# The second feed-forward product of a three-mixer block: from four full block products to seven, summed over the pairs of inner tiles

## The chip, the cores and the metric

One core of one Trainium2 chip runs the whole kernel. The metric is device time in microseconds (us) of one execution. The engines are PE (TensorE, matmuls), DVE (VectorE), ACT (ScalarE), POOL (GpSimd) and SP (SyncE, which here only issues DMAs). Each engine works through its own instructions in a fixed order, so an instruction that waits holds up all that stand behind it on that engine.

## The reference, cut to what matters

The kernel computes one layer of a hybrid backbone. The change touches its last part, the feed-forward block and the norm behind it (`lat` has 1024 tokens of 1024 channels; the hidden width is 2816):

```
def swiglu(xn, w_in, w_out):
    gate, up = jnp.split(xn @ w_in, 2, axis=-1)
    return (jax.nn.silu(gate) * up) @ w_out
...
h_lat = h_lat + gt2l * swiglu(modulate(rms_norm(h_lat, norm2), sh2l, sc2l), w_ffn_in, w_ffn_out)
...
return rms_norm(h_lat, norm_f)
```

The product by `w_in` is called the first product here, the one by `w_out` the second. The second is (1024 x 2816) by (2816 x 1024).

## The kernel before

Matmuls run on fp32r operands. To keep fp32 accuracy each operand is split into a high part (ACT writes a rounded copy, L1670) and a low part (DVE subtracts the copy from the raw tile, L1671), and each product of two tiles is three matmuls: high by high, high by low, low by high. One matmul is 128 x 128 by 128 x 512 and fills or adds to one of eight PSUM banks (tile `mm`).

`ffn_in` makes the hidden tensor, transposed: a tile is 128 hidden channels by 512 tokens. It goes by pairs of hidden tiles (11 pairs), and already uses a seven-product scheme for its own 2 x 2 blocks: per pair 2 x 7 products of 12 matmuls, gate and up. `done` applies SiLU to the gate tiles (L1598, ACT) and multiplies up by gate (L1601, POOL); `hidden(i, g)` sends the four finished tiles of pair i to the DRAM tensor `hid_d` (L1589, issued on SP). `g[j, h]` is hidden tile j of the pair and token half h.

`ffn_out` makes the second product. It loops over the two token halves h; in each half, for every one of the 22 hidden tiles k, it loads the hidden tile (L1676, tile `hraw`, four buffers) and the weight rows (L1681, tile `wraw`, 128 x 1024), splits the hidden tile into `hk` (six buffers) and the two weight halves into `wk` (`wt` for the first four k of the first half), and issues 24 matmuls (L1718): 4 token tiles t by 2 column halves n by 3. All eight banks are in use in a half. The weights are thus loaded and split twice. In the last two k the order is turned to t and n outside, k inside, so that the banks finish one after the other, and `out` follows each: multiply by the gate row `bc1` (L1689, DVE), add the residual (L1691, POOL, the last token tile on DVE), sum of squares (L1693, ACT), and after the second column half the root (L1699, L1700, POOL), the final norm (L1704, DVE) and the store (L1705).

The order on each engine comes from a scheduler at build time; pools hand out buffers, and DMAs are issued in program order on SP's queue, each waiting there for its buffer or its data. Pools are opened on the right side as others close, so the first tiles of `ffn_out` lie where `ffn_in` kept its data.

Of the kernel before, what the change touches and what calls it, by code (L numbers as in the profile page):

```python
# [16 lines left out]
P = 128  # L17
# [1076 lines left out]
RK, WK, HK = 4, 6, 6  # L1094
HR, WR = 4, 4
# [16 lines left out]
class Kern(LruMixin, S5Mixin, RwkvMixin, ParamMixin, SplitMixin):  # L1112
# [546 lines left out]
    def ffn_out(s, ring, wpool, apool, hpool, pa):  # L1659


        nc = s.nc
# [11 lines left out]
        def hidden(k, h):
            raw = hpool.tile([P, 512], F32, name="hraw", tag="hraw", bufs=HR)
            nc.sync.dma_start(raw, s.hid_d[k, h])  # L1676
            return operand(raw, hpool, "hk", HK)

        def weights(k, first):
            raw = pa.tile([P, D], F32, name="wraw", tag="wraw", bufs=WR)  # L1680
            nc.sync.dma_start(raw, s.i["w_ffn_out"][0][P * k : P * k + P, :])  # L1681
            pool, tag, bufs = (ring, "wt", 8) if first and k < RK else (wpool, "wk", 2 * WK)
            return [operand(raw[:, 512 * n : 512 * n + 512], pool, tag, bufs) for n in range(2)]

        def out(h, t, n, ps, rs):
            j = 4 * h + t
            at = lambda n: acc[:, j, 512 * n : 512 * n + 512]
            v = pa.tile([P, 512], F32, name="ot", tag="ot", bufs=4)
            V.tensor_tensor(v, ps, bc1[:, 512 * n : 512 * n + 512], op=ALU.mult)  # L1689
            a = at(n)  # L1690
            (V if h and t == 3 else G).tensor_tensor(a, a, v, op=ALU.add)  # L1691
# [290 lines left out]
```

## Time and profile before

| what | value |
| --- | --- |
| median of 3 runs | 2331.59 us (2330.96 to 2336.67) |
| the profiled execution's own time | 2331.55 us |
| its span in the profile | 2329.8 us |
| mean granted TensorE clock | 0.952 |

The profile shows one execution, with its times counted from the start of the span; the execution's own time is 1.75 us longer than the span. A busy time is the time in which an engine had at least one instruction under way. Idle time is put down to the releaser that came last.

### The profile page before, as it was taken

Reading aid. Unit: us, or ns where it says so; the run is one execution under the profiler, and the core shown is the slowest. Engines: PE = TensorE matmul, PEld = TensorE weight load, DVE = VectorE, ACT = ScalarE, POOL = GpSimd, SP = SyncE. Lnnn points to the kernel's source line nnn. Section 1 sums busy time; section 2 is a strip of 40 time slices with the busy share of each in tenths; the row PEclk is TensorE's granted clock in tenths of the full one; section 3 lists DMA queues with packets and bytes.
Section 4 is the critical chain, followed back from the end, with each engine's and each line's share of the span. In section 5 each row is a group of like instructions: output and inputs, shape, how many; then the busy total and the mean of one; then the engine's idle time right before and its main releaser. Section 6 shows DMA issues by size and latency. Waiting matters only on the chain.

```text
span 2329.8 us, 38390 instructions
## 1 busy us (share of the span) xinstructions
PE 2102.5 (90%) x14573; PEld 1675.7 (72%) x14573; DVE 1508.0 (65%) x2218; ACT 904.2 (39%) x1698; POOL 986.0 (42%) x1169
## 2 busy tenths in 40 slices
PE   5979988887899988898699999898999999989998
PEld 3868866665778877776467676676788888878886
DVE  5656698889566888899843366936855555543533
ACT  5313354423334645454533333416433323233431
POOL 3662389955323494856100122544644444300302
PEclk8989999998999999998699999998999999999999
DMA  6634322221663535445967777544222222274540
GB/s 254 168 110 115 90 66 83 82 84 64 143 174 89 161 111 140 125 136 142 246 181 173 171 191 183 167 158 136 81 77 86 77 86 77 68 276 151 165 149 36
DMA packets 360550, 307.26 MB, mean 132 GB/s; under 512 B 66023, under 2 KB 311982, under 8 KB 359342
## 3 DMA queue, kind: packets, MB, share of 16 engines
q1 hardware_dynamic: 356782, 293.27, 43.5%
q10 hardware_dynamic: 2880, 10.49, 1.2%
q8 instruction: 115, 1.88, 0.3%
q0 software_dynamic: 704, 1.05, 0.2%
q14 instruction: 69, 0.57, 0.1%
HBM read 219.03 MB, written 85.70 MB: 131 GB/s over the span
## 4 chain that ended last, share of the span: by engine, by line
PE 56%; DVE 19%; POOL 9%; DMA 7%; issue 5%; ACT 3%; SPq 1%; DVEq 0%; POOLq 0%; ACTq 0%
PE mm L1563 18%; PE mm L1718 10%; PE mm L1303 8%; PE mm L1309 7%; PE cg L1011 2%; PE cg L985 2%; PE cu L998 2%; DMA wm<-in_w_mod_dram 1%; DVE zl L1296 1%; PE cy L1026 1%; POOL s L214 1%; DVE s5ct L522 1%; PE aux L609 1%; DVE macc L1269 1%; DVE rn L748 1%
## 5 line engine op out<-in xcount | busy, mean ns | idle before, releaser
L1563 PE MATMUL mm<-q,wt 128*128 128x512 f32 x1584 | 376.6, 398 | 4.5 <-DVE q L1477 3.2
L1563 PEld LDWEIGHTS mm<-q,wt 128*128 128x128 f32 x1584 | 299.4, 189 | 77.5 <-DVE q L1477 3.6
L1718 PE MATMUL mm<-wk,hk 128*128 128x512 f32 x960 | 224.2, 396 | 0.0
L1303 PE MATMUL mm<-xh,wh 128*128 128x512 f32 (+1 forms) x576 | 214.4, 380 | 8.4 <-ACT ya L180 6.1
L1303 PE MATMUL mm<-xl,wh 128*128 128x512 f32 (+1 forms) x576 | 214.3, 379 | 1.2 <-DVE xl L1219 1.2
L1718 PEld LDWEIGHTS mm<-wk,hk 128*128 128x128 f32 x960 | 180.4, 188 | 43.6
L1309 PE MATMUL mm<-xh,zh 128*128 128x512 f32 x384 | 159.6, 416 | 10.0 <-ACT zge L1345 5.8
L1309 PE MATMUL mm<-xl,zh 128*128 128x512 f32 x384 | 159.5, 415 | 0.0
L1303 PE MATMUL mm<-xh,wl 128*128 128x512 f32 (+1 forms) x576 | 141.2, 383 | 8.8 <-DVE wl L1296 6.6
L1303 PEld LDWEIGHTS mm<-xh,wh 128*128 128x128 f32 x576 | 114.3, 199 | 28.6 <-ACT ya L180 6.9
L1671 DVE TENSOR_TENSOR wk<-wraw,wk 128x512 fp32r<-128x512 f32 x80 | 55.9, 707 | 111.3 <-ACT wk L1670 111.3
L1303 PEld LDWEIGHTS mm<-xl,wh 128*128 128x128 f32 x576 | 113.8, 197 | 19.4 <-DVE xl L1219 1.5
L1309 PE MATMUL mm<-byt,bwh 128*128 128x512 f32 x384 | 118.6, 428 | 7.9 <-ACT bwh L1295 2.9
L1303 PEld LDWEIGHTS mm<-xh,wl 128*128 128x128 f32 x576 | 102.9, 197 | 30.1 <-DVE wl L1296 8.2
L1309 PE MATMUL mm<-xh,zl 128*128 128x512 f32 x384 | 110.1, 423 | 15.3 <-DVE zl L1296 15.3
L1691 POOL TENSOR_TENSOR acc<-acc,ot 128x512 f32<-128x512 f32 x14 | 19.0, 1358 | 225.7 <-DVE ot L1689 225.2
L1015 DVE TENSOR_TENSOR x<-cg,pcend 64x256 f32<-64x256 f32 x152 | 63.9, 421 | 77.9 <-PE cg L1011 35.4
L1476 ACT ACTIVATE wt<-wT 128x512 fp32r<-128x512 f32 x88 | 55.1, 631 | 142.5 <-PE mm L1563 130.5
L1309 PEld LDWEIGHTS mm<-xh,zl 128*128 128x128 f32 x384 | 75.4, 202 | 35.2 <-DVE zl L1296 18.3
L1269 DVE SCALAR_TENSOR_TENSOR macc<-wm,cs,macc 128x256 f32<-128x256 f32 x112 | 84.6, 755 | 22.3 <-DMA wm<-in_w_mod_dram 19.8
L1477 DVE TENSOR_TENSOR wt<-wt 128x512 fp32r<-128x512 f32 x66 | 60.5, 918 | 59.4 <-ACT wt L1476 59.0
L1293 POOL CAST bwh<-bwr 128x512 fp32r<-128x512 f32 x16 | 10.0, 624 | 209.6 <-PE mm L1309 112.1
(421 smaller groups left out, 4865.3 us busy)
## 6 DMA issues: line engine op xcount, KB each, us to landing
wt<-in_w_ffn_in_dram SPq DMA_DIRECT2D x44, 512.0 KB
wraw<-in_w_ffn_out_dram SPq DMA_DIRECT2D x44, 512.0 KB
wm<-in_w_mod_dram SPq DMA_DIRECT2D x64, 256.0 KB
gyl<-gyl SPq DMA_DIRECT2D x32, 512.0 KB
wr<-in_w_in_dram SPq DMA_DIRECT2D x27, 512.0 KB
zr<-in_w_in_dram SPq DMA_DIRECT2D x24, 512.0 KB
sgd<-zge SPq DMA_DIRECT2D x48, 256.0 KB
bsg<-sgd SPq DMA_DIRECT2D x48, 256.0 KB
```

Source lines behind the costliest of these rows:

```text
L985: s.pe = nc.tensor.matmul(ps[32 * q : 32 * q + 32, 64 * p : 64 * p + 64], gy[:, 2 * p + par, c - cb, 0:32], st["x"][:, p, par, :], start=T ...
L998: s.pe = nc.tensor.matmul(ps[o : o + 32, 64 * p : 64 * p + 64], st["tt"][32 * q : 32 * q + 32, p, st["cc"], :], st["gs"][32 * q : 32 * q + ...
L1011: s.pe = nc.tensor.matmul(sn[64 * par : 64 * par + 64, 64 * p : 64 * p + 64], sd[:, st["cc"], 2 * p + par, :], st["x"][:, p, par, :], star ...
L1015: V.tensor_tensor(xn[0:64, :, par, :], sn[r].rearrange("p (a k) -> p a k", a=4), vb(s.pcend[r, d, :, st["c"]], 64), op=ALU.mult)
L1269: nc.vector.scalar_tensor_tensor(acc, wm[:, j], s.cs[:, k + j, 0:1], acc, op0=ALU.mult, op1=ALU.add)
L1303: s.nc.tensor.matmul(ps, w(k), a(k), start=n == 0, stop=n == len(seq) - 1)
L1309: s.nc.tensor.matmul(ps, w[:, k], a[:, k], start=n == 0, stop=n == len(seq) - 1)
L1476: s.nc.scalar.activation(hi, raw, AF.Copy)
L1477: (eng or s.nc.vector).tensor_tensor(lo, raw, hi, op=ALU.subtract)
L1563: nc.tensor.matmul(ps, w[:, k], a[:, k], start=n == 0, stop=n == len(seq) - 1)
L1671: V.tensor_tensor(hl[:, 1], raw, hl[:, 0], op=ALU.subtract)
L1718: nc.tensor.matmul(banks[t, n], a[:, tk], b, start=k == 0 and q == 0, stop=k == NF - 1 and q == 2)
```

## The change

`hidden` now sends seven tiles per pair instead of four: a11, a12, a21, a22 (first index token half, second index tile of the pair) and the sums a21 = a21 + a22, f2 = a21 - a11, f0 = a11 - a21 (before the sum), f1 = a12 - f2. The sums overwrite the gate tiles, which are kept for it (`g` holds both now). Two of the four extra operations are POOL's, two DVE's.

`ffn_out` runs seven products c = 0 to 6. Each multiplies one kind of hidden tile with one kind of weight block (128 x 512) over the 11 pairs k, for 4 token tiles t, three matmuls each, in four banks. The even c share one set of four banks and the odd c the other. Products 2, 4 and 6 are added to what the set holds. The 44 raw weight blocks are loaded once, each into its own buffer; the differences that products 1, 2, 4 and 6 need are made in place by POOL (`sub`). The split of operands moves to `split2` (L1475 on ACT, L1476 on DVE), all weight operands go through the `wt` ring (eight buffers), and the last two pairs of a product have t outside. `done(c, t)` takes a finished bank into `acc`; products 3 to 6 finish one quarter of the output each, for which `out` loads the residual itself (`xr`, two buffers, on SP; before it was loaded into `acc` on ACT's queue).

```diff
-            for (j, h), v in g.items():
-                nc.sync.dma_start(s.hid_d[2 * i + j, h], v)
+            (a11, f0), (a12, f1), (a21, _), (a22, f2) = g[0, 0], g[1, 0], g[0, 1], g[1, 1]
+            G.tensor_tensor(f0, a11, a21, op=ALU.subtract)
+            V.tensor_tensor(a21, a21, a22, op=ALU.add)
+            V.tensor_tensor(f2, a21, a11, op=ALU.subtract)
+            G.tensor_tensor(f1, a12, f2, op=ALU.subtract)
+            for c, v in enumerate((a11, a21, f2, a12, f0, f1, a22)):
+                nc.sync.dma_start(s.hid_d[c, i], v)
...
+        def block(k, j, n):
+            w = raw[k, j, n] = wpool.tile([P, 512], F32, name="wraw", tag=f"w{j}{n}{k}")
+            r = 2 * P * k + P * j
+            nc.sync.dma_start(w, s.i["w_ffn_out"][0][r : r + P, 512 * n : 512 * n + 512])
+            return w
...
+            if c == 0:
+                return block(k, 0, 0)
+            if c == 1:
+                return sub(w(0, 0), block(k, 0, 1), w(0, 0))
+            if c == 2:
+                return sub(w(0, 0), block(k, 1, 1), w(0, 0))
+            if c == 3:
+                return block(k, 1, 0)
+            if c == 4:
+                return sub(w(0, 1), w(1, 1), w(0, 1))
+            if c == 5:
+                return w(1, 1)
+            return sub(w(0, 0), w(1, 0), w(0, 0))
...
+        def out(h, n, t, v):
+            a, j = acc[:, h, n, t], 4 * h + t
+            x = pa.tile([P, 512], F32, name="xr", tag="xr", bufs=2)
+            nc.sync.dma_start(x, s.x2_d[j, :, 512 * n : 512 * n + 512])
+            E = V if (h, n) == (1, 0) else G
+            E.tensor_tensor(a, v, bc1[:, 512 * n : 512 * n + 512], op=ALU.mult)
+            (V if (h, n, t) == (1, 0, 3) else G).tensor_tensor(a, a, x, op=ALU.add)
...
+        def done(c, t):
+            ps = banks[c % 2][t]
+            if c < 2:
+                S.activation((o11, o21)[c][t], ps, AF.Copy)
+            elif c == 2:
+                S.activation(o12[t], ps, AF.Copy)
+                G.tensor_tensor(o12[t], o12[t], o21[t], op=ALU.add)
+            elif c == 3:
+                V.tensor_tensor(o11[t], o11[t], ps, op=ALU.add)
+                out(0, 0, t, o11[t])
+            elif c == 4:
+                S.activation(o22[t], ps, AF.Copy)
+                G.tensor_tensor(o22[t], o22[t], o21[t], op=ALU.add)
+                out(1, 1, t, o22[t])
+            elif c == 5:
+                V.tensor_tensor(o12[t], o12[t], ps, op=ALU.add)
+                out(0, 1, t, o12[t])
+            else:
+                out(1, 0, t, ps)
...
+        for c in range(7):
+            ops = []
+            def matmuls(k, t):
+                a, b = ops[k]
+                for q, (i, j) in enumerate(((0, 0), (0, 1), (1, 0))):
+                    nc.tensor.matmul(banks[c % 2][t], a[:, i, P * t : P * t + P], b[:, j],
+                                     start=c in (0, 1, 3, 5) and k == 0 and q == 0,
+                                     stop=c in (1, 3, 5, 6) and k == NK - 1 and q == 2, skip_group_check=True)
+            for k in range(NK):
+                ops.append((hidden(c, k), operand(weights(c, k), ring, "wt", 8)))
+                if k < NK - LK:
+                    for t in range(4):
+                        matmuls(k, t)
+            for t in range(4):
+                for k in range(NK - LK, NK):
+                    matmuls(k, t)
+                done(c, t)
```

The first place where instructions move is SP's queue at the passage from the first to the second product (`hidd` is `hid_d`; a wait names the engine or DMA lane waited for). Before:

```order
L1676 DMA hraw<-hidd 128x512 [waits DMAHW1_49,DVE_49]
L1676 DMA hraw<-hidd 128x512 [waits DMAHW3_49,DVE_49]
L1676 DMA hraw<-hidd 128x512 [waits DMAHW4_49,DVE_49]
L1589 DMA hidd<-ft 128x512 [waits Pool_49] x2
L1589 DMA hidd<-ft 128x512 [waits DMAHW5_49,Pool_49]
L1681 DMA wraw<-in_w_ffn_out_dram 128x1024 [waits DMAHW6_49,PE_49]
L1681 DMA wraw<-in_w_ffn_out_dram 128x1024 [waits DMAHW7_49,PE_49]
L1681 DMA wraw<-in_w_ffn_out_dram 128x1024 [waits DMAHW0_49]
L1681 DMA wraw<-in_w_ffn_out_dram 128x1024 [waits DMAHW1_49]
L1681 DMA wraw<-in_w_ffn_out_dram 128x1024 [waits DMAHW6_49,DMAHW2_49,DVE_49]
```

After, SP's queue at the same place:

```order
L1709 DMA hraw<-hidd 128x512 [waits DMAHW2_49,DVE_49]
L1593 DMA hidd<-ft 128x512 [waits Pool_49]
L1593 DMA hidd<-ft 128x512 [waits DMAHW0_49,Pool_49]
L1593 DMA hidd<-ft 128x512 [waits DVE_49]
L1593 DMA hidd<-ft 128x512 [waits Pool_49]
L1593 DMA hidd<-ft 128x512 [waits DMAHW3_49,DVE_49]
L1593 DMA hidd<-ft 128x512 [waits DMAHW4_49,Pool_49]
L1679 DMA wraw<-in_w_ffn_out_dram 128x512 [waits DMAHW6_49,PE_49]
L1679 DMA wraw<-in_w_ffn_out_dram 128x512 [waits DMAHW7_49]
L1679 DMA wraw<-in_w_ffn_out_dram 128x512 [waits DMAHW1_49]
L1679 DMA wraw<-in_w_ffn_out_dram 128x512 [waits DMAHW2_49]
```

Six hidden tiles of the last pair now stand ahead of the first weight load, where it was three, and the last of them waits for POOL.

The second place is POOL at the same passage; L1601 and L1605 are the products of up by gate. Before:

```order
L1601 TENSOR_TENSOR ft<-ft 128x512 [waits DMAHW2_49,DVE_49]
L1601 TENSOR_TENSOR ft<-ft 128x512 [waits DMAHW7_49,DVE_49]
L1601 TENSOR_TENSOR ft<-ft 128x512 [waits DMAHW5_49,DVE_49]
L1601 TENSOR_TENSOR ft<-ft 128x512 [waits DMAHW3_49,DVE_49,Activation_49]
L1601 TENSOR_TENSOR ft<-ft 128x512 [waits DMAHW2_49,DVE_49,Activation_49]
L1601 TENSOR_TENSOR ft<-ft 128x512 [waits DMAHW7_49,DVE_49,Activation_49]
L1691 TENSOR_TENSOR acc_18920<-acc_18920,ot 128x512 [waits DMAHW3_49,DVE_49]
L1691 TENSOR_TENSOR acc_18920<-acc_18920,ot 128x512 [waits DVE_49]
```

After (L1588 is f0, L1591 is f1, L1683 is `sub`, with the numbers of the weight tiles):

```order
L1588 TENSOR_TENSOR ft_18414<-ft_18555,ft_18599 128x512 [waits Pool_49]
L1605 TENSOR_TENSOR ft_18635<-ft_18635,ft_18494 128x512 [waits DMAHW6_49,DVE_49]
L1591 TENSOR_TENSOR ft_18494<-ft_18635,ft_18476 128x512 [waits DMAHW2_49,DVE_49,Pool_49]
L1605 TENSOR_TENSOR ft_18848<-ft_18848,ft_18707 128x512 [waits DVE_49]
L1605 TENSOR_TENSOR ft_18910<-ft_18910,ft_18769 128x512 [waits DMAHW5_49,DVE_49,Activation_49]
L1605 TENSOR_TENSOR ft_18892<-ft_18892,ft_18751 128x512 [waits DMAHW6_49,DVE_49,Activation_49]
L1588 TENSOR_TENSOR ft_18707<-ft_18848,ft_18892 128x512 [waits DMAHW7_49,Pool_49]
L1605 TENSOR_TENSOR ft_18928<-ft_18928,ft_18787 128x512 [waits DMAHW7_49,DVE_49,Activation_49]
L1591 TENSOR_TENSOR ft_18787<-ft_18928,ft_18769 128x512 [waits DMAHW3_49,DVE_49,Pool_49]
L1683 TENSOR_TENSOR wraw_19016<-wraw_19262,wraw_19016 128x512 [waits DMAHW2_49,DMAHW6_49,DVE_49,PE_49]
L1683 TENSOR_TENSOR wraw_19038<-wraw_19285,wraw_19038 128x512 [waits DMAHW7_49,DMAHW3_49,DVE_49]
L1683 TENSOR_TENSOR wraw_19060<-wraw_19308,wraw_19060 128x512 [waits DMAHW4_49,DMAHW1_49,DVE_49]
```

One more operation, f1, stands behind the last product of up by gate, and POOL goes on with weight differences where it had nothing to do until the first token half ended.

The third place is POOL at the end of the program, from the last additions of the residual on (`st` and `rs` are the sums of squares and the root). Before:

```order
L1696 TENSOR_SCALAR rs_20632<-st_18925 128x1 [waits Activation_49]
L1691 TENSOR_TENSOR acc_18920<-acc_18920,ot 128x512 [waits DMAHW1_49,DVE_49]
L1699 TENSOR_SCALAR rs_20632<-st_18925,rs_20632 128x1 [waits Activation_49,Pool_49]
L1691 TENSOR_TENSOR acc_18920<-acc_18920,ot 128x512 [waits DVE_49]
L1700 TENSOR_TENSOR rs_20632<-rs_20632,mhalf 128x1 [waits Pool_49]
L1696 TENSOR_SCALAR rs_20660<-st_18925 128x1 [waits Activation_49]
L1699 TENSOR_SCALAR rs_20660<-st_18925,rs_20660 128x1 [waits Activation_49,Pool_49]
L1700 TENSOR_TENSOR rs_20660<-rs_20660,mhalf 128x1 [waits Pool_49]
L1696 TENSOR_SCALAR rs_20688<-st_18925 128x1 [waits Activation_49]
L1699 TENSOR_SCALAR rs_20688<-st_18925,rs_20688 128x1 [waits Activation_49,Pool_49]
L1700 TENSOR_TENSOR rs_20688<-rs_20688,mhalf 128x1 [waits Pool_49]
```

After:

```order
L1719 TENSOR_TENSOR acc_18997<-acc_18997,xr 128x512 [waits DMAHW2_49,DVE_49]
L1719 TENSOR_TENSOR acc_18997<-acc_18997,xr 128x512 [waits DMAHW4_49,DVE_49]
L1728 TENSOR_SCALAR rs_20274<-st_19002,rs_20274 128x1 [waits Activation_49]
L1729 TENSOR_TENSOR rs_20274<-rs_20274,mhalf 128x1 [waits Pool_49]
L1719 TENSOR_TENSOR acc_18997<-acc_18997,xr 128x512 [waits DMAHW4_49,DVE_49]
L1728 TENSOR_SCALAR rs_20290<-st_19002,rs_20290 128x1 [waits Activation_49]
L1729 TENSOR_TENSOR rs_20290<-rs_20290,mhalf 128x1 [waits Pool_49]
L1728 TENSOR_SCALAR rs_20306<-st_19002,rs_20306 128x1 [waits Activation_49]
L1729 TENSOR_TENSOR rs_20306<-rs_20306,mhalf 128x1 [waits Pool_49]
L1728 TENSOR_SCALAR rs_20322<-st_19002,rs_20322 128x1 [waits Activation_49]
L1729 TENSOR_TENSOR rs_20322<-rs_20322,mhalf 128x1 [waits Pool_49]
```

Each token tile has one addition on POOL now instead of two (the last tile's is DVE's, as before): the first two stand ahead of all roots, the third behind the first root, and the first half of each root's sum was made earlier, in product 4.

## Rows read from the trace of the kernel before

**Rows 1.** The page: span, busy time, share and instructions of each engine.

```profile
span 2329.8 us, 38390 instructions
PE 2102.5 (90%) x14573; PEld 1675.7 (72%) x14573; DVE 1508.0 (65%) x2218; ACT 904.2 (39%) x1698; POOL 986.0 (42%) x1169
```

**Rows 2.** Busy time by stretch; its first row names the columns.

```profile
core 0: us, PE busy (x) PEld busy (x) DVE busy (x) ACT busy (x) POOL busy (x), PEclk, DMA share, GB/s
1900.00:1940.00 40.00, 40.00 (x174) 32.28 (x173) 22.07 (x30) 12.81 (x22) 18.27 (x13) 1.00 0.24 79
2020.00:2070.00 50.00, 44.09 (x190) 35.29 (x188) 18.69 (x28) 9.62 (x16) 10.10 (x8) 0.97 0.38 124
2070.00:2100.00 30.00, 29.03 (x118) 23.25 (x119) 15.44 (x24) 13.95 (x24) 0.00 (x0) 0.93 1.01 395
2100.00:2130.00 30.00, 30.00 (x131) 24.14 (x130) 11.19 (x17) 10.72 (x18) 0.00 (x0) 1.00 0.39 135
2319.00:2330.00 11.00, 0.14 (x1) 0.00 (x0) 6.89 (x11) 2.07 (x6) 5.57 (x8) 0.70 0.51 191
```

**Rows 3.** Groups from 2020 us on: busy, mean ns, idle before, releaser.

```profile
L1718 PE MATMUL mm<-wk,hk 128*128 128x512 f32 x960 | 224.2, 396 | 0.0
L1718 PE MATMUL mm<-wt,hk 128*128 128x512 f32 x96 | 24.2, 415 | 6.9 <-ACT wt L1670 6.9
L1671 DVE TENSOR_TENSOR wk<-wraw,wk 128x512 fp32r<-128x512 f32 x80 | 55.9, 707 | 111.3 <-ACT wk L1670 111.3
L1691 POOL TENSOR_TENSOR acc<-acc,ot 128x512 f32<-128x512 f32 x14 | 19.0, 1358 | 225.7 <-DVE ot L1689 225.2
L1704 DVE SCALAR_TENSOR_TENSOR acc<-acc,rs,bcr 128x512 f32<-128x512 f32 x16 | 13.0, 854 | 1.2 <-POOL rs L1700 1.2
```

**Rows 4.** The chain that ended last, from 1900 us: start, length, what.

```profile
1899.89 163.60 PE mm L1563 x704
2064.95 1.27 POOL ft L1601
2066.66 3.55 DMA wraw<-in_w_ffn_out_dram
2070.28 0.64 ACT wt L1670
2070.97 239.78 PE mm L1718 x1020
```

**Rows 5.** Timeline between the two products: start, length, instruction, idle before.

```profile
2047.39 1.75 SPq L1676 DMA_DIRECT2D hraw<-hidd  x4
...
2050.05 0.63 ACT L1670 ACTIVATE hk<-hraw 128x512 fp32r<-128x512 f32 x1 [2.06 <-DMA hraw<-hidd]
...
2061.19 2.90 PE L1563 MATMUL mm<-s,wt 128*128 128x512 f32 x12
2070.97 9.23 PE L1718 MATMUL mm<-wt,hk 128*128 128x512 f32 x32 [6.88 <-ACT wt L1670]
```

**Rows 6.** Timeline where DVE and POOL run without a pause.

```profile
1678.61 3.48 DVE L1477 TENSOR_TENSOR wt<-wt 128x512 fp32r<-128x512 f32 x2
1679.80 3.44 POOL L1601 TENSOR_TENSOR ft<-ft 128x512 f32<-128x512 f32 x2
1682.01 0.68 DVE L1619 TENSOR_TENSOR ft<-fe,mm 128x512 f32<-128x512 f32 x1
1684.20 1.29 POOL L1610 TENSOR_TENSOR wT<-wt 128x512 f32<-128x512 f32 x1 [0.96 <-DMA wt<-in_w_ffn_in_dram]
```

**Rows 7.** Timeline of POOL between two pairs of the first product.

```profile
1908.58 1.28 POOL L1601 TENSOR_TENSOR ft<-ft 128x512 f32<-128x512 f32 x1 [1.01 <-DVE ft L1642]
1911.78 1.82 POOL L1610 TENSOR_TENSOR wT<-wt 128x512 f32<-128x512 f32 x1 [1.92 <-ACT wt L1476]
```

**Rows 8.** Timeline of the end.

```profile
2299.61 19.53 PE L1718 MATMUL mm<-wk,hk 128*128 128x512 f32 x83
...
2325.19 1.41 DVE L1704 SCALAR_TENSOR_TENSOR acc<-acc,rs,bcr 128x512 f32<-128x512 f32 x2 [0.71 <-POOL rs L1700]
```

More of the change, by code (lines that the diff above doesn't have):

```diff
@@ L1093 @@
 WTB = 6
-RK, WK, HK = 4, 6, 6
-HR, WR = 4, 4
+HR, HK, LK = 4, 6, 2
 WSEQ = "w n0 w n1 n2 n3 f s0 f s1 f s2 f f s3"
@@ L1674, in hidden @@
[L1674 to L1691, printed above, removed]
+        raw = {}
+        def block(k, j, n):
[3 more added lines that the diff above has]
+            return w
@@ new lines, in operand, with hidden @@
+        def operand(x, pool, tag, bufs):
+            hl = pool.tile([P, 2, 512], F32R, name=tag, tag=tag, bufs=bufs)
+            s.split2(x, (hl[:, 0], hl[:, 1]))
+            return hl
+        def hidden(c, k):
+            x = hpool.tile([P, 512], F32, name="hraw", tag="hraw", bufs=HR)
+            nc.sync.dma_start(x, s.hid_d[c, k])
+            return operand(x, hpool, "hk", HK)
+        def out(h, n, t, v):
[5 more added lines that the diff above has]
+            (V if (h, n, t) == (1, 0, 3) else G).tensor_tensor(a, a, x, op=ALU.add)
@@ L1703, in out @@
                 sl = slice(512 * n, 512 * n + 512)
-                V.scalar_tensor_tensor(at(n), at(n), r, bc2[:, sl], op0=ALU.mult, op1=ALU.mult)
-                nc.sync.dma_start(s.out[0][tt : tt + P, sl], at(n))
+                V.scalar_tensor_tensor(acc[:, h, n, t], acc[:, h, n, t], r, bc2[:, sl], op0=ALU.mult, op1=ALU.mult)
+                nc.sync.dma_start(s.out[0][tt : tt + P, sl], acc[:, h, n, t])
         rs = {}
-        for h in range(2):
-            banks = {}
-            ops = {}
-            def matmuls(k, t, n):
-                (hh, hl), (wh, wl) = ops[k][0], ops[k][1][n]
-                tk = slice(P * t, P * t + P)
-                if (t, n) not in banks:
-                    banks[t, n] = s.mm()
-                for q, (a, b) in enumerate(((hh, wh), (hh, wl), (hl, wh))):
-                    nc.tensor.matmul(banks[t, n], a[:, tk], b, start=k == 0 and q == 0, stop=k == NF - 1 and q == 2)
-            for k in range(NF):
-                ops[k] = hidden(k, h), weights(k, h == 0)
-                if h == 0 and 2 <= k < 10:
-                    with s.tc.issue_after(s.last.ins):
-                        nc.scalar.dma_start(acc[:, k - 2], s.x2_d[k - 2])
-                if k < NF - 2:
@@ new lines, in ffn_out @@
+        banks = [[s.mm() for t in range(4)] for b in range(2)]
+        o11, o12, o21, o22 = ([acc[:, h, n, t] for t in range(4)] for h in range(2) for n in range(2))
+        def done(c, t):
[17 more added lines that the diff above has]
+                out(1, 0, t, ps)
@@ L1726, in ffn_out @@
                     for t in range(4):
-                        for n in range(2):
-                            matmuls(k, t, n)
+                        matmuls(k, t)
             for t in range(4):
-                for n in range(2):
-                    for k in (NF - 2, NF - 1):
-                        matmuls(k, t, n)
-                    out(h, t, n, banks[t, n], rs)
+                for k in range(NK - LK, NK):
+                    matmuls(k, t)
+                done(c, t)
     def drams(s, dr):
```

29 lines of the change are left out of this document (16 added, 13 removed).

## The prediction

> **What bounds the kernel now.** I read the page first: PE is busy in 90% of the span and the next engine, DVE, in 65% [rows 1]. That is a mean over many stages, so I went to the table by stretch for the stage that the change touches. From 1900 us on PE is busy for all of every stretch at a granted clock of 1.00, through the first product and the second, while DVE, ACT and POOL stay far below (DVE 22 of 40 us in the first product, 11 of 30 in the second) [rows 2]. Only two places differ: the passage between the products and the last 11 us. The chain of waits says the same: 163.60 us of matmuls of the first product, a short passage, 239.78 us of matmuls of the second, then the tail [rows 4]. So a matmul that goes away here comes off the time, as long as the other engines keep PE fed.
>
> The second product runs from 2070.97 us [rows 5] to 2299.61 + 19.53 = 2319.14 us [rows 8], 248.17 us for 960 + 96 = 1056 matmuls [rows 3]. Its first 32 took 9.23 us [rows 5], in a stretch with a clock of 0.93 [rows 2]; at the pace of the first product, 163.60 / 704 = 0.2324 us [rows 4], they would take 7.44. So 1.8 us is the price of the start after the idle passage, and the steady pace is (248.17 - 1.8) / 1056 = 0.2333 us a matmul. The 396 ns of one matmul [rows 3] is a length with overlap and no price.
>
> **The change, part by part.** *Matmuls.* Before 1056, after 7 products x 11 pairs x 4 token tiles x 3 = 924. The shape is the same, and so is the order within three. 132 fewer x 0.2333 = **-30.8 us**, and the stage would take 217.4 us. A bank that is added to costs PE nothing that a row shows: every matmul but the first of a bank adds already. Banks change hands without a wait: product c + 2 needs the set that `done(c)` read a whole product, 132 x 0.2333 = 30.8 us, earlier.
>
> *Operands.* Before 44 hidden and 88 weight splits; after 77 and 77, 154. On ACT one is 0.63 us [rows 5], 22 per product 13.9 us of 30.8. On DVE one is 0.71 us when POOL is quiet [rows 3], 15.6 us of 30.8. Both fit. But POOL is not quiet any more. It gets 44 weight differences, and by `done` 35 more 128x512 operations (4 for product 2, 8, 12 and 8 for 3 to 5, 3 for 6). Where both engines run without a pause, two POOL operations took 3.44 us and the two splits of DVE beside them 3.48 [rows 6], that is a pair in 1.74 us, against 1.29 for POOL alone [rows 6] and 0.71 for DVE alone [rows 3]. A DVE operation that reads a bank kept its 0.68 us [rows 6]. So POOL's work stretches DVE's splits, at worst each one that it meets by 1.03 us. The dense part is products 0 to 2, where all 44 differences stand ahead of everything else on POOL: 44 x 1.74 + 22 x 0.71 = 92.2 us for DVE's 66 splits, against 3 x 30.8 = 92.4 of PE. That is just enough, and DVE begins with a lead (six hidden and eight weight operand buffers, some 12 splits). In the whole stage at most 79 splits can meet a POOL operation: 79 x 1.74 + 75 x 0.71 = 190.7, and 16 final-norm operations x 0.85 [rows 3] and 13 that read banks x 0.68 make it 213 of 217.4. I take **0** for starving, and keep +3 to +11 for it below.
>
> The Trainium skill ("SBUF — State Buffer", section "SBUF: two separate sides") says that such a DVE operation with two SBUF inputs and a GpSimd operation that reads SBUF hold the shared port pair exclusively, each for the whole instruction. By it the pair would cost the sum of both. The trace agrees in kind (the bank-reading operation is spared), and its pair is shorter than that sum.
>
> *Loads.* The weights come once: 44 x 256 KB for 44 x 512 KB; hidden tiles are 77 for 44, and 16 residual loads move from ACT's queue, where they fell into the start, to SP. In the start stretch DMA moved 395 GB/s [rows 2]. After, the first 33 us need at most 44 + 12 tiles of 256 KB, 14.7 MB, about 37 us at that rate, but product 0 itself uses one weight block in 2.8 us and its blocks come first. SP's in-order waits for POOL (residual buffers) stand ahead of hidden loads only in products 4 to 6; with up to ten hidden tiles ahead, 28 us of matmuls, a wait of a few us there is covered. **0**.
>
> *First product.* Four more operations per pair: 2 on DVE, 2 on POOL, plus three 256 KB writes. After a pair POOL had 1.92 us idle before the next pair's first weight sum [rows 7], and f0 fits before the last product of up by gate, f1 (1.29 us) behind it. PE there never waits, with eight banks to fill. **0**; if the cover were gone, f0 and f1 would cost 2 x 1.3 x 11 = 29 us, which I give no weight because PE had other products ready.
>
> *Passage.* PE idles from 2061.19 + 2.90 = 2064.09 to 2070.97, 6.88 us [rows 5]. The steps: last bank drained by DVE, last product of up by gate on POOL until 2066.22, its store, then the first weight load, issued at 2066.66 and landed after 3.55 us, ACT 0.64, PE [rows 4]. After, f1 stands between: +1.3 us on POOL, and its store on SP, +0.3 with it. The sums on DVE run beside the last POOL product. The load is 256 KB instead of 512; a 256 KB tile on an idle queue took from 2047.39 to 2050.05 = 2.66 us [rows 5], the large one 3.55, so it gains 0 to 0.9. I take -0.4: **+1.2 us**, range +0.7 to +1.6.
>
> *Tail.* From 2319.14 to the span's end at 2329.8 [rows 1] is 10.7 us, with the last norm operations on DVE from 2325.19 to 2326.6 [rows 8]. After, the last four token tiles finish every 6 x 0.233 = 1.4 us instead of 2.8, so all four queue up behind the last matmul: DVE has four products by the gate, one addition and eight norm operations, 5 x 0.7 + 8 x 0.85 = 10.3 us, of which three products lie before the last matmul: some 8.2 us after it if POOL's roots keep pace, against 2326.6 - 2319.14 = 7.5 before. The third and fourth residual loads wait for a buffer that POOL frees by the first two additions: issued about 2 us and 0.6 us before the last matmul ends, 2.66 us each, so the third addition starts up to 1 us late. I take **+1.0**, range 0 to +3.
>
> Sum: -30.8 + 0 + 0 + 0 + 1.2 + 1.0 = -28.6. The profiled execution took 2331.55 us, 1.75 more than its span, and is within 0.1 us of the median 2331.59. 2331.55 - 28.6 = **2303.0 us**, 1.2% faster. What a measurement of this kernel can tell from no change is about 0.3%, 7 us.
>
> **The rivals.** *Starved in products 0 to 2.* If POOL and DVE cannot overlap at all, a pair costs 1.29 + 0.71 = 2.0 us: 44 x 2.0 + 22 x 0.71 = 103.6 us against 92.4, 11 us short, of which the lead of 12 splits (8.5 us) may hide most. Time 2306 to 2314. For it: the margin above is only 0.2 us. Against: pairs of 1.74 in the trace, and many POOL operations will wait for a DVE split and so not be dense. The rule of the Trainium skill's page named above ("SBUF — State Buffer") describes this mechanism; the times here are from rows alone.
>
> *The first weight loads wait for stores.* If the buffers behind the first blocks are free only when the last stores have landed, the passage grows by another 2.66 us: 2306. For it: the buffers lie where the first product worked. Against: before, the load was issued 0.44 us after POOL's last product (2066.66 - 2066.22), with that product's store in between, so it did not wait for the store to land [rows 4].
>
> *Slower.* DVE becomes the bound of the whole stage. Without the 22.5 us of its other operations it has 217.4 - 22.5 = 195 us for 154 splits, so this begins at a mean split of 1.27 us, and the gain is gone at (195 + 28.6) / 154 = 1.45. At 1.74 for every split the stage takes 154 x 1.74 + 22.5 = 290 us, 73 more, 2376. Against: it needs more POOL operations than the 79 there are; with 79 met the mean is 1.24.
>
> *No gain.* PE waits 22 us or more somewhere, say by f0 and f1 in each pair (29 us above): about 2332. Against: PE's idle is 0 in that stage, with POOL busy 18 of 40 us [rows 2].
>
> **How the numbers follow.** Forecast (2300 to 2306) 0.72; starved 0.14; loads behind stores 0.07; no gain 0.04; slower 0.03. The range 2299.5 to 2313 takes in the first three: the low end is no cost at either end of the stage (2300.7) and a little of the start's 1.8 us back. All up to 2324.6 count as faster: 0.93; same 0.04; slower 0.03.
>
> **What would show it.** Right: 924 matmuls at 0.233 us, a stage of 217 to 218 us, PE without idle in it, a first split mean of DVE near 1.0 us in products 0 to 2, a passage of about 8 us and a tail of about 11.7. Starving: PE waiting for DVE `wt` or `hk` in the first 90 us of the stage. Stores: the first `wraw` issued more than 1 us after f1's store. Wrong altogether: PE idle in the first product, or a pace other than 0.233 us.

## The result, and the profile after

The changed kernel took 2304.48 us (median of four runs, 2302.47 to 2308.66) beside 2331.28 us for the kernel before: a ratio of 0.9882, 95% interval 0.9861 to 0.9904, so 1.2% faster. The forecast was 2303.0. The profiled execution took 2306.05 us, with a span of 2304.3. The page of after, beside [rows 1]:

```profile
span 2304.3 us, 38442 instructions
PE 2076.8 (90%) x14441; PEld 1655.4 (72%) x14441; DVE 1623.4 (70%) x2257; ACT 923.4 (40%) x1736; POOL 1129.0 (49%) x1256
```

PE has 132 matmuls and 25.7 us less; POOL has 143 us more, DVE 115. Where these fall is seen by stretch (columns as in [rows 2]):

```profile
2070.00:2100.00 30.00, 25.56 (x103) 20.57 (x104) 23.32 (x20) 13.43 (x23) 18.10 (x11) 0.87 1.03 375
2100.00:2130.00 30.00, 29.52 (x127) 23.33 (x126) 30.00 (x19) 13.01 (x23) 30.00 (x19) 1.00 0.50 165
2130.00:2160.00 30.00, 30.00 (x131) 24.13 (x130) 30.00 (x23) 15.14 (x27) 25.59 (x16) 1.00 0.37 106
```

DVE and POOL have no pause between 2100 and 2130 us, and PE is still fed, nearly. The groups of the second product (columns as in [rows 3]; line 1766 the matmuls, 1476 DVE's part of a split, 1683 the weight differences) tell the same:

```profile
L1766 PE MATMUL mm<-wt,hk 128*128 128x512 f32 x924 | 217.8, 398 | 10.6 <-ACT wt L1475 10.1 <-DVE hk L1476 0.5
L1476 DVE TENSOR_TENSOR wt<-wraw,wt 128x512 fp32r<-128x512 f32 x77 | 93.6, 1224 | 7.0 <-ACT wt L1475 6.9
L1476 DVE TENSOR_TENSOR hk<-hraw,hk 128x512 fp32r<-128x512 f32 x77 | 81.0, 1059 | 29.8 <-ACT hk L1475 29.7
L1683 POOL TENSOR_TENSOR wraw<-wraw 128x512 f32<-128x512 f32 x44 | 74.5, 1725 | 17.4 <-DMA wraw<-in_w_ffn_out_dram 13.0 <-DVE wt L1476 4.4
```

A split took 1224 and 1059 ns in the mean, where it took 707 before [rows 3]. PE was idle for 10.1 us ahead of the first matmul, and for 0.5 us once inside the stage. Idle time of PE inside the stage is called starving below. On the timeline PE's second product is two pieces:

```profile
2074.44 48.27 PE L1766 MATMUL mm<-wt,hk 128*128 128x512 f32 x199 [10.12 <-ACT wt L1475]
2123.19 169.49 PE L1766 MATMUL mm<-wt,hk 128*128 128x512 f32 x725 [0.48 <-DVE hk L1476]
```

The stage ends at 2123.19 + 169.49 = 2292.68 us and took 218.24 us, against 248.17 before: -29.93. The last 11.62 us to the span's end, the tail, were 10.66 before: +0.96. The passage, where [rows 5] had 6.88 us of idle PE, has 10.12: +3.24. Here is its timeline (line 1605 is POOL's product of up by gate, 1590 and 1591 the sums f2 and f1, 1441 a row load, 1679 the weight loads):

```profile
2061.42 2.90 PE L1562 MATMUL mm<-s,wt 128*128 128x512 f32 x12
...
2065.18 1.74 POOL L1605 TENSOR_TENSOR ft<-ft 128x512 f32<-128x512 f32 x1
2065.84 1.63 DVE L1590 TENSOR_TENSOR ft<-ft 128x512 f32<-128x512 f32 x1
2067.22 0.33 ACTq L1441 DMA_DIRECT2D bcr<-in_norm_f_dram  x1
2067.61 1.26 POOL L1591 TENSOR_TENSOR ft<-ft 128x512 f32<-128x512 f32 x1 [0.68 <-POOL ft L1605]
2069.31 6.03 SPq L1679 DMA_DIRECT2D wraw<-in_w_ffn_out_dram  x10
2073.76 1.31 ACT L1475 ACTIVATE wt<-wraw 128x512 fp32r<-128x512 f32 x2 [15.62 <-DMA wraw<-in_w_ffn_out_dram]
```

With the +0.23 us by which the first product ended later, the terms give 0.23 + 3.24 - 29.93 + 0.96 = -25.5, the difference of the spans.

One more row is needed to compare runs. Whole times of this same kernel lay between 2296.15 and 2308.66 us in the run above and its repeats below. Where that stands can be seen in the three of them that were profiled: their spans differ by 4.4 us, and all but 0.7 of it stands ahead of the first product, in code that no edit touches. The view of one line gives the first and the last start of its matmuls (ahead of them the shortest, median and longest length in ns):

```profile
L1562 PE MATMUL mm<-q,wt x1584: 388/395/795, 1625.9 to 2061.2; 128*128 128x512 f32 x198
```

In the kernel before the same line gives 1626.0; in the runs below it starts between 1618.3 and 1627.0. So, beside medians, I compare the time from this start to the end of the span, called **the rest** here: 703.8 us before (2329.8 - 1626.0), 678.4 after.

### The profile page after: what moved, and what is told of

Its sections match the earlier page's. It is cut to its first block, busy times and chain, and to the rows that moved or that the text cites. A ratio compares the mean times of both kernels' runs of the same rounds, so it can differ in the third digit from the quotient of the medians.

```text
span 2304.3 us, 38442 instructions
## 1 busy us (share of the span) xinstructions
PE 2076.8 (90%) x14441; PEld 1655.4 (72%) x14441; DVE 1623.4 (70%) x2257; ACT 923.4 (40%) x1736; POOL 1129.0 (49%) x1256
## 4 chain that ended last, share of the span: by engine, by line
PE 54%; DVE 22%; DMA 8%; POOL 6%; issue 5%; ACT 3%; SPq 1%; DVEq 0%; ACTq 0%; POOLq 0%
PE mm L1562 18%; PE mm L1766 9%; PE mm L1302 7%; PE mm L1308 7%; PE cg L1011 3%; PE cg L985 2%; PE cu L998 2%; DMA wm<-in_w_mod_dram 2%; DVE macc L1268 2%; DVE zl L1295 1%; DVE xc L140 1%; PE cy L1026 1%; POOL s L214 1%; DVE s5ct L522 1%; PE aux L609 1%
## 5 line engine op out<-in xcount | busy, mean ns | idle before, releaser
L1766 PE MATMUL mm<-wt,hk 128*128 128x512 f32 x924 | 217.8, 398 | 10.6 <-ACT wt L1475 10.1
L1766 PEld LDWEIGHTS mm<-wt,hk 128*128 128x128 f32 x924 | 174.5, 189 | 53.8 <-ACT wt L1475 10.5
L1302 PEld LDWEIGHTS mm<-xh,wl 128*128 128x128 f32 x576 | 101.5, 194 | 25.5 <-DVE wl L1295 5.5
L1475 ACT ACTIVATE wt<-wT 128x512 fp32r<-128x512 f32 x88 | 55.0, 631 | 141.0 <-PE mm L1562 129.0
L1476 DVE TENSOR_TENSOR hk<-hraw,hk 128x512 fp32r<-128x512 f32 x77 | 81.0, 1059 | 29.8 <-ACT hk L1475 29.7
L1002 ACT ACTIVATE x<-cu 32x256 f32<-32x256 f32 x156 | 58.5, 375 | 102.0 <-PE cu L998 99.0
L1476 DVE TENSOR_TENSOR wt<-wraw,wt 128x512 fp32r<-128x512 f32 x77 | 93.6, 1224 | 7.0 <-ACT wt L1475 6.9
```

Of the source, the lines that this page charges most:

```text
L1002: S.activation(st["x"][96:128, :, par, :], ps[o : o + 32, 0:256].rearrange("p (a k) -> p a k", a=4), AF.Copy)
L1302: s.nc.tensor.matmul(ps, w(k), a(k), start=n == 0, stop=n == len(seq) - 1)
L1475: s.nc.scalar.activation(hi, raw, AF.Copy)
L1476: (eng or s.nc.vector).tensor_tensor(lo, raw, hi, op=ALU.subtract)
L1766: nc.tensor.matmul(banks[c % 2][t], a[:, i, P * t : P * t + P], b[:, j], start=c in (0, 1, 3, 5) and k == 0 and q == 0, stop=c in (1, 3, 5 ...
```

## The experiments

All have the changed kernel as their base. Three profiles of it, the one above and two repeats, give a rest of 678.4, 677.7 and 678.4 us, a passage of 10.12, 10.09 and 10.03, starving of 0.48, 0.53 and 0.48, and a tail of 11.62, 10.93 and 11.65; the mean rest is 678.2. Every rest below is one profiled run beside this mean, so a difference under 0.7 us says nothing.

> The changed kernel itself, beside the other runs of this call. It shows how far runs of it lie apart: from the first product's start to the end 678.4 us within 0.5 us, and where the whole time differs by more, the difference stands before that start (1618 to 1626 us so far).

Measured: 2304.0 us (0.9891, 0.9873 to 0.991), rest 677.7, which is 0.7 us from the first where 0.5 was expected.

> The changed kernel once more beside the run above, for a comparison on one chip: 677.5 to 678.5 us from the first product's start, and a whole time 4 to 6 us above the run above.

Measured: 2303.25 us (0.9888, 0.987 to 0.9906), rest 678.4; 4.2 us above the run beside it.

**Is a product's price its matmuls?**

```
-        for c in range(7):
+        for i, c in enumerate((0, 1, 2, 3, 4, 5, 5, 6)):
...
-                done(c, t)
+                if i != 5:
+                    done(c, t)
```

> Product 5 is made twice, its first result is dropped: 924 + 132 = 1056 matmuls, as many as before the change; the hidden sums, the weight differences and the order of the rest stay. Theory A (the gain is the 132 matmuls at TensorE's pace): +30.8 us, 132 x 0.2333, so 2335 us, some 4 us above the kernel before, which is what the passage and the tail cost. Rival B (part of the gain is that lanes or loads are relieved): the extra product costs another sum, under 28 or over 34 us.

Measured: 2335.52 us (1.0023, 1.0013 to 1.0034 of before), rest 709.1, +30.9. PE's timeline:

```profile
2067.60 48.01 PE L1766 MATMUL mm<-wt,hk 128*128 128x512 f32 x199 [10.09 <-ACT wt L1475]
2116.18 200.28 PE L1766 MATMUL mm<-wt,hk 128*128 128x512 f32 x857 [0.57 <-DVE hk L1476]
```

The second piece is 857 matmuls in 200.28 us, 0.2337 each, as the 725 in 169.49 above are 0.2338. Theory A holds. With as many matmuls as before the change, the kernel is 0.2% slower than before, by the rest 5.3 us (709.1 - 703.8). That is the price of the passage (+3.2), the tail (+1.3) and the starving (0.6).

**What do the weight differences cost?**

```
-            G.tensor_tensor(o, a, b, op=ALU.subtract)
             return o
```

> Left out: the 44 weight differences that POOL forms in products 1, 2, 4 and 6 (the undifferenced block is split and multiplied instead). Everything else stands. Theory A (the lock-step with POOL is hidden behind PE): POOL's 44 differences lengthen VectorE's splits from about 0.7 to 1.78 us in products 0 to 2, but PE waited only 0.5 us for a split in the profile after, so without them the stage loses at most that: 0 to -2 us, 2302 to 2305 us, while VectorE's busy share of 2100:2160 falls from full to some 75%. Rival B (the stage is starved in most runs, and the 6 us between the fastest and the slowest run after is that): the time falls by 2 to 6 us and the spread shrinks to under 1 us. The passage (10.1 us of idle TensorE) stays by both, since its differences are those of the hidden tiles.

Measured: 2303.74 us (0.99, 0.9886 to 0.9915), rest 677.8, 0.4 us less; PE runs the stage in one piece:

```profile
2071.52 217.82 PE L1765 MATMUL mm<-wt,hk 128*128 128x512 f32 x924 [10.18 <-ACT wt L1475]
```

Splits fell to 857 and 800 ns (DVE was busy for 48% of 2100 to 2160, where 75% was expected), and the time hardly moved: theory A. The runs still spread from 2302.67 to 2308.32, so the spread is not the starving, against B.

The opposite, each difference made twice, was meant to price the lock-step:

```
+            x = pa.tile([P, 512], F32, name="ot", tag="ot", bufs=4)
+            G.tensor_tensor(x, a, b, op=ALU.subtract)
             G.tensor_tensor(o, a, b, op=ALU.subtract)
```

> Each of the 44 weight differences is formed twice on POOL, the first time into a scratch tile; results as before. Times are compared from the first matmul of the first feed-forward product (678.4 us to the end of the profile after), since that start moved from 1618 to 1626 us between runs of unlike kernels that are the same up to there. Theory A (POOL and VectorE go in lock-step, 1.74 us for a pair, and VectorE is at its limit in products 0 to 2): 88 POOL operations take more VectorE time than there is, TensorE waits for splits of line 1476, the stage grows by 8 to 16 us from 218.2. Rival B (VectorE's full windows are work done ahead of need): 0 to +2 us. Rival C (one excludes the other entirely): over +20 us.

Measured: 2354.23 us (1.011, 1.0091 to 1.0129 of before), rest 729.2, +51. It doesn't decide between the three. The 44 weight blocks leave no room for a scratch tile of its own, so it shares four buffers with the squares of the outputs, and half of the differences were made only behind the outputs of products 3 and 5. The place behind product 3:

```profile
2213.54 1.27 POOL L1684 TENSOR_TENSOR ot<-wraw 128x512 f32<-128x512 f32 x1
2213.62 0.63 ACT L1475 ACTIVATE wt<-wraw 128x512 fp32r<-128x512 f32 x1 [6.14 <-POOL wraw L1685]
2214.30 2.07 PE L1768 MATMUL mm<-wt,hk 128*128 128x512 f32 x4 [16.31 <-ACT wt L1475]
```

PE waited 16.31 us here and 19.37 us ahead of product 6, for POOL itself. In products 0 to 2, where POOL so had the same 44 operations as in the changed kernel, the idle pieces sum to 2.0 us for 0.5. What it does show: a difference that comes late is paid in full, and more. The idle pieces of the stage sum to 41.6 us, and the stage grew by 50.75 (268.99 for 218.24): behind the two long waits PE also ran at a lower granted clock, 0.57 from 2214 to 2220 us and 0.54 from 2299 to 2305, for 1.00 in the stretch that follows each.

**What is the passage made of?** First without the hidden sums:

```
-            G.tensor_tensor(f0, a11, a21, op=ALU.subtract)
-            V.tensor_tensor(a21, a21, a22, op=ALU.add)
-            V.tensor_tensor(f2, a21, a11, op=ALU.subtract)
-            G.tensor_tensor(f1, a12, f2, op=ALU.subtract)
```

> Left out: the four sums and differences over the pairs of hidden tiles (the seven stores send the tiles unsummed), in all eleven pairs. Theory A (the passage is as long as it is because the last pair's chain f2, f1 and its store stand ahead of the first weight load on SP's queue): the last store goes some 3.0 to 3.7 us earlier, when the last hidden product is done, and the passage falls from 10.1 to about 7 us: -2 to -4 us, 2300 to 2303 us. Rival B (the loads' landing behind the two row loads and the stores is what lasts): the weight load starts earlier but lands as late, 0 to -1 us. First product: no change by both, since TensorE had no idle time in 1900:1940 after either.

Measured: 2298.56 us (0.987, 0.9854 to 0.9885), rest 676.4; the passage is 8.92 us. The residual loads (line 1712) and PE's second product:

```profile
2059.03 0.87 SPq L1712 DMA_DIRECT2D xr<-x2d  x2
2065.37 218.29 PE L1762 MATMUL mm<-wt,hk 128*128 128x512 f32 x924 [8.92 <-ACT wt L1475]
```

The first weight load was issued 3.50 us after PE's last matmul instead of 4.99 (2069.31 - 2064.32), but landed after 4.7 us behind two residual loads that had moved ahead of it. The last store went 2.4 us sooner against PE's last matmul, and 0.9 of it was lost to issuing those two loads. So each theory had half: the chain gave 1.5 us, the landing took 0.3 back.

Then with the row loads late:

```
+            if c == 2:
+                with s.tc.issue_after(s.last.ins):
+                    bc[:] = [s.row_bc_to(...) for j in (1, 2)]
```

> The two row loads of 512 KB on ScalarE's queue (line 1441, issued at 2060.35 and 2067.22 us in the profile after) are issued only when product 1 is done; results as before. Theory A (the first weight load lands after 4.43 us, not 3.55, because the row loads move beside it): the load lands in 3.0 to 3.6 us and the passage falls from 10.1 to 9.0 to 9.5 us; the time to the end from the first product's start falls by about 1 us. Rival B (twelve weight loads share the transfer engines and slow the first): the passage stays within 0.3 us of 10.1. By both the third product's scaling on POOL waits for nothing new, since product 3 ends some 65 us later.

Measured: 2302.72 us (0.989, 0.9873 to 0.9908), rest 676.2. The first load and what waited for it:

```profile
2070.38 5.35 SPq L1679 DMA_DIRECT2D wraw<-in_w_ffn_out_dram  x11
2073.65 1.20 ACT L1475 ACTIVATE wt<-wraw 128x512 fp32r<-128x512 f32 x2 [14.24 <-DMA wraw<-in_w_ffn_out_dram]
2074.33 218.01 PE L1769 MATMUL mm<-wt,hk 128*128 128x512 f32 x924 [8.94 <-ACT wt L1475]
```

It was issued as late as before (4.99 us after PE's last matmul), but it took 3.19 us to land, not 4.43, and the passage is 8.94. Theory A. The rest fell by 2.0 us, twice what A gave it: the passage is 1.1 of that, the starving went too (0.5), and the tail was 10.86, near the 10.93 of a repeat.

**Can the passage go?** The first four weight blocks get buffers that are free early:

```
+            pool = hpool if (j, n) == (0, 0) and k < 4 else wpool
-            w = raw[k, j, n] = wpool.tile(...)
+            w = raw[k, j, n] = pool.tile(...)
```

> The first four blocks of the second product's weights get buffers in the pool of the hidden tiles, which is free before the first product ends, so their loads stand ahead of the last six stores on SP's queue; results as before. Theory A (the passage is the chain of the last hidden sums, their stores, and the weight load queued behind them): the first four pairs of operands are ready when the first product ends, TensorE has 48 matmuls (11.0 us at 0.229) to cover the chain, and the passage falls from 10.1 to under 1.5 us: the time from the first product's start falls by 8 to 10 us. Rival B (the wait only moves to the fifth weight block, whose buffer is free no sooner and which lands among twelve loads): the first idle stretch vanishes but a second of 3 to 7 us stands 10 us later, and the gain is 3 to 6 us.

Measured: 2302.64 us (0.9889, 0.9869 to 0.9908), rest 677.3. PE's timeline, and DVE and POOL by stretch:

```profile
2062.59 3.89 PE L1767 MATMUL mm<-wt,hk 128*128 128x512 f32 x16
2067.84 7.74 PE L1767 MATMUL mm<-wt,hk 128*128 128x512 f32 x32 [1.36 <-DVE wt L1476]
2077.83 3.07 PE L1767 MATMUL mm<-wt,hk 128*128 128x512 f32 x12 [2.26 <-ACT wt L1475]
2081.30 31.58 PE L1767 MATMUL mm<-wt,hk 128*128 128x512 f32 x134 [0.40 <-ACT wt L1475]
2114.89 3.06 PE L1767 MATMUL mm<-wt,hk 128*128 128x512 f32 x12 [2.01 <-DVE hk L1476]
2118.27 4.47 PE L1767 MATMUL mm<-wt,hk 128*128 128x512 f32 x18 [0.32 <-DVE hk L1476]
2125.04 5.63 PE L1767 MATMUL mm<-wt,hk 128*128 128x512 f32 x23 [2.30 <-DVE hk L1476]
2131.82 30.59 PE L1767 MATMUL mm<-wt,hk 128*128 128x512 f32 x130 [1.15 <-DVE hk L1476]
2163.04 127.89 PE L1767 MATMUL mm<-wt,hk 128*128 128x512 f32 x547 [0.63 <-DVE hk L1476]
```

```profile
2100.00:2130.00 30.00, 25.37 (x107) 19.44 (x106) 30.00 (x18) 10.98 (x20) 30.00 (x19) 1.00 0.63 223
2130.00:2160.00 30.00, 28.85 (x124) 22.91 (x124) 30.00 (x19) 13.32 (x26) 30.00 (x18) 1.00 0.34 93
```

The passage fell to 1.36 + 2.26 + 0.40 = 4.02 us, 6.1 less, and starving rose to 2.01 + 0.32 + 2.30 + 1.15 + 0.63 = 6.41, 5.9 more. Both theories missed this: the gain is had and given back 50 us later. PE begins earlier, but the first difference was made 25.3 us after PE's first matmul (2087.9 us), against 7.5 in the changed kernel (2081.9). It waits for weight loads, and these come later: the fifth block's load went out 10.15 us after the first product's last matmul, where the first went out 4.99 us after it in the changed kernel. So the splits that POOL holds up meet products that stand earlier. Both the earlier start and the later loads have a part in this, and no run tells them apart. If the held splits are the cause, the starving must go with the differences:

> The early weights of the run before last but one, and with them the 44 weight differences left out (the undifferenced blocks are multiplied). With early weights alone TensorE's idle time at the passage fell to 4.0 us in three pieces, and 6.4 us of new idle time came at 2112 to 2163 us, while VectorE and POOL had 30.00 of 30 us busy. Theory A (VectorE, held by POOL's differences, was just fed in the changed kernel, because the 10.1 us of the passage gave it a head start; without this start it starves TensorE): without the differences the 6.4 us are gone, and from the first product's start to the end it takes 670.5 to 671.5 us, against 677.3 with early weights alone. Rival B (the starving comes of the transfers, which run at a share of 1.05 in 2080 to 2100, and late hidden tiles): 3 us or more of it stay, 674 to 677 us.

Measured: 2301.59 us (0.988, 0.9861 to 0.9899), rest 672.8. PE and then the same two stretches:

```profile
2066.84 7.73 PE L1766 MATMUL mm<-wt,hk 128*128 128x512 f32 x32 [1.34 <-DVE wt L1476]
2079.25 206.21 PE L1766 MATMUL mm<-wt,hk 128*128 128x512 f32 x876 [4.67 <-ACT wt L1475]
```

```profile
2100.00:2130.00 30.00, 30.00 (x130) 24.15 (x129) 14.36 (x22) 14.65 (x25) 0.00 (x0) 1.00 0.77 266
2130.00:2160.00 30.00, 30.00 (x131) 24.14 (x130) 14.23 (x22) 14.76 (x26) 1.23 (x1) 1.00 0.34 95
```

The 6.41 us are gone, as A says. The rest is 1.3 us above its range: the fifth weight block, issued at 2071.90 us, was split only at 2078.56, 6.66 us later, where it was 4.26 us in the run before (2072.89 to 2077.15). The two row loads were issued beside it in both; what made the difference was not settled.

**Can both go?** The differences are held back: those for product 2 until product 0 is done, those for 4 and 6 until product 2 is done.

```
-                return sub(w(0, 0), block(k, 1, 1), w(0, 0))
+                return sub(w(0, 0), block(k, 1, 1), w(0, 0), s.p0)
...
-                return sub(w(0, 1), w(1, 1), w(0, 1))
+                return sub(w(0, 1), w(1, 1), w(0, 1), s.p2)
...
-            return sub(w(0, 0), w(1, 0), w(0, 0))
+            return sub(w(0, 0), w(1, 0), w(0, 0), s.p2)
```

> The changed kernel, where the differences for product 2 are formed only after product 0, those for products 4 and 6 only after product 2; results as before, and the same number of operations. Theory A (the lock-step costs the changed kernel next to nothing, since the passage hides it): 0 to -0.7 us from the first product's start (677.7 and 678.4 so far), and VectorE's busy time in 2100 to 2160 falls below 60.0 of 60 us. Rival B (the held-back differences come in a bunch and starve the third and fourth product): +1 to +6 us, TensorE's idle time between 2165 and 2230 us.

Measured: 2307.3 us (0.9907, 0.9889 to 0.9925), rest 680.5, +2.3: rival B. The place:

```profile
2220.93 1.29 POOL L1721 TENSOR_TENSOR acc<-acc,xr 128x512 f32<-128x512 f32 x1 [3.94 <-DMA xr<-x2d]
2223.89 0.63 ACT L1724 ACTIVATE ot<-acc 128x512 f32<-128x512 f32 x1 [0.92 <-POOL acc L1721]
2224.52 0.61 ACT L1476 ACTIVATE hk<-hraw 128x512 fp32r<-128x512 f32 x1
2225.19 3.38 PE L1770 MATMUL mm<-wt,hk 128*128 128x512 f32 x8 [1.71 <-ACT hk L1476]
```

The outputs of product 3 are late on POOL, one of their additions waits for its residual load, ACT's square waits for the addition, and the next split stands behind that square in ACT's queue. PE waits 1.71 us, and the 0.5 us of starving in product 1 are gone, so the wait alone doesn't give +2.3. The rest of it is PE's pace: its granted clock was 0.66 from 2225 to 2230 us, and the last 285 matmuls took 68.57 us, 0.2406 each for 0.2338, which is 1.9 us; the tail of 10.84 takes some of it back.

With early weights and late row loads added:

> Early weights, spread differences and late row loads together; results as before. Theory A (the passage was both the cost of the chain and the cover of VectorE, so each edit alone gives 0 to 1.5 us and together they give the sum): idle time at the passage 2 to 4 us, none from 2100 to 2290, 668.5 to 671.5 us from the first product's start, 2293 to 2297 us in all. Rival B (the fifth weight block's load, which waits for the last product and stands among twelve, lasts): the passage keeps 4 us and the differences of product 1 still starve the first 40 us by 3 us: 673 to 675 us.

Measured: 2300.57 us (0.9877, 0.9858 to 0.9895), rest 673.9:

```profile
2065.09 7.73 PE L1774 MATMUL mm<-wt,hk 128*128 128x512 f32 x32 [1.36 <-DVE wt L1477]
2076.11 41.47 PE L1774 MATMUL mm<-wt,hk 128*128 128x512 f32 x170 [3.29 <-ACT wt L1476]
2118.00 98.51 PE L1774 MATMUL mm<-wt,hk 128*128 128x512 f32 x421 [0.41 <-DVE hk L1477]
2217.75 67.02 PE L1774 MATMUL mm<-wt,hk 128*128 128x512 f32 x285 [1.24 <-ACT hk L1476]
```

The passage is 4.65 us, 5.4 less, and 1.65 us of other idle time is 1.2 more; -4.3 in the rest. Early weights gave 0.9 us alone, late row loads 2.0, held differences -2.3, which adds up to 0.6; together they give 4.3. A's range was missed by 2.4 us. The 3.29 us for the fifth block are the wait of B, whose starving of 3 us was 0.41. Last, the differences for product 4 already after product 1 (`s.p1` in place of `s.p2`):

> All three edits, with the differences laid out eleven to a product: those for product 2 after product 0, for product 4 after product 1, for product 6 after product 2; results as before. In the run with all three, 1.24 us of idle time stood at 2217.75 us, where ScalarE's split stood behind a square that waited for POOL's additions of product 3's outputs, which the 22 differences after product 2 had made late. Theory A (it is the bunching): that piece goes, the passage keeps 4 to 5 us, 672 to 673 us from the first product's start (673.9 with the bunch, 677.7 and 678.4 in the changed kernel). Rival B (the 22 to 33 differences now at hand in products 0 to 2 starve TensorE there again): 1 to 4 us of idle time between 2090 and 2165 us, 674 to 677 us.

Measured: 2299.05 us (0.987, 0.9849 to 0.9891), rest 674.2:

```profile
2070.41 7.73 PE L1775 MATMUL mm<-wt,hk 128*128 128x512 f32 x32 [1.36 <-DVE wt L1477]
2080.14 40.26 PE L1775 MATMUL mm<-wt,hk 128*128 128x512 f32 x170 [2.00 <-ACT wt L1476]
2122.41 8.11 PE L1775 MATMUL mm<-wt,hk 128*128 128x512 f32 x27 [2.01 <-DVE hk L1477]
2130.87 158.69 PE L1775 MATMUL mm<-wt,hk 128*128 128x512 f32 x679 [0.36 <-DVE hk L1477]
```

The piece at 2217 us went and 2.37 us of starving came, so each theory has half, though the passage of 3.36 us is shorter than A's 4 to 5. The two versions can't be told apart by the rest (673.9 and 674.2). Both take some 4 us less than the changed kernel by it, and the last one 4.2 by medians on the chip that ran both (2299.05 and 2303.25). By whole times alone that isn't shown: the runs overlap, and so do the intervals against the kernel before.

## Why the prediction was right, point by point

The terms add up to -28.6 us. The profiled pair gave -25.5 and the medians -26.8, so the sum is 3.1 us off: 2.0 in the passage, 0.9 in the stage, 0.2 in a first product that ended later. That the whole time came within 1.5 us of the forecast is in part luck, since single runs of this kernel lie up to 12.5 us apart.

- **Matmuls, -30.8: right.** The stage fell by 29.93 us, with 0.48 us of starving in it, and the eighth product put back costs 30.9 us. The gain is PE's own time.
- **Starving, 0: nearly right, for a reason that was not all there.** It was 0.5 us. The working had 92.2 us of DVE against 92.4 of PE and six hidden and eight weight buffers of lead. That was near: 70 splits kept DVE busy for 90.3 of the 92.6 us of products 0 to 2, 1.29 us each (41 filled the 60 us from 2100 to 2160, 1.46 each). The sign "near 1.0 us" did not fit the working itself, where 92.2 / 66 is 1.40. What the working left out is when the differences begin against PE's start. With early weights PE starts at once and the differences later; the same work then starves it for 6.4 us, and without the differences for none. So the term came out near 0 with some luck: the margin is almost used up, and the 10 us of the passage, which the working didn't count, are part of it.
- **First product, 0: right.** From the line's first to its last start it is 435.0 us before (1626.0 to 2061.0) and 435.3 after. "PE there never waits" holds from 1900 us on; at the start of the stage PE stood idle for 4.5 us before and 5.0 after, none of it for POOL.
- **Passage, +1.2: the term that was mis-sized, by 2.0 us.** It measured +3.24. The load was issued 2.42 us later against PE's last matmul (4.99 for 2.57), where the step had +1.6. f1's 1.26 us is there, but the last product of up by gate and f2 met on POOL and DVE, 1.74 us for 1.27, and POOL then stood 0.68 us. The three make up the 2.42. The step let the sums on DVE run beside the last POOL product at no cost, and so left out the slowing of the two engines by each other that the paragraph on operands had found. And the landing, put at -0.4, was +0.88: 4.43 us for half the bytes. Before, the two row loads of 512 KB went out ahead of the passage:

```profile
2057.58 0.33 ACTq L1442 DMA_DIRECT2D bcr<-gtd  x1
2057.94 0.46 ACTq L1442 DMA_DIRECT2D bcr<-in_norm_f_dram  x1
```

  Their tiles now come from another pool (`pa` for `apool`; the diff shown ahead of the prediction doesn't have this line), and the second went out at 2067.22, beside the weight loads. The diff moves them and the prediction did not follow them; with the row loads held back, the weight load lands in 3.19 us.
- **Tail, +1.0: right in the profiled run** (+0.96); the repeats give 10.93 and 11.65 us, so +0.3 to +1.0 against the one profile of the kernel before.
- **Rivals.** The first weight load was issued 0.42 us after f1's store (2068.89), so it waited for no store. No gain and slower did not come: the sums added no idle time to the first product (0.5 us more, at its start), and the mean split was 1.14 us, below the 1.27 at which DVE would set the pace. Starved in products 0 to 2 did not come either. Its condition, a pair at 2.0 us, did not hold: 32 differences in a row took 54.29 us, 1.70 each. But the wait that it names is the one that early weights brought out.

## What to carry to other kernels

Where PE was the bound, the matmuls removed came off the time one for one, and the price lay in the joints: follow every transfer whose buffer the diff moves to another pool, not only the ones whose lines it edits. An idle stretch ahead of a stage can be the cover of another engine's work: before paying to close it, look at which engine is full just behind it, or the gain is handed over, as 6.1 us were for 5.9 here. And a short wait of PE can cost more than its length, as the 1.71 us did with the differences held back.

## What the hardware did that was not expected

- While POOL forms differences without a pause, DVE runs one split per POOL operation: 36 of each in the 60 us from 2100 to 2160 with early weights (in the two lines above an operation that crosses 2130 stands in both), against 44 of DVE in 28.59 us with POOL all but idle (without the differences). The Trainium skill ("SBUF — State Buffer", section "SBUF: two separate sides") has a DVE operation with two SBUF inputs and a GpSimd operation that reads SBUF hold a shared port pair exclusively, each for the whole instruction. In kind this is so; but 36 splits at 0.69 us and 36 POOL operations at 1.26, their lengths in quiet stretches, would be 70.2 us in turn, and they took 60.0. The measurement decides: part of the two overlaps.
- Waits of PE of nearly the same length had unlike prices. Behind 1.71 us (held differences) the granted clock was 0.66 from 2225 to 2230 us, and behind 2.01 us (the last run) 0.67 from 2122 to 2127; with early weights it stayed at 1.00 from 2100 to 2160, through waits of 2.01 and 2.30 us. What decides is open.
- The same code ahead of the first product took 1618.3 to 1627.0 us in runs of these kernels. What in it varies was not looked for and stays open; it is larger than most effects here, and the start of the first product is the better zero for them.
